# Row variance on one core: one row pitch for all loads, the first load at the head of SP's list

## The chip, the cores and the metric

The kernel runs on one core of a Trainium2 chip. The metric is the device time of one execution in microseconds; the median of several runs stands for a kernel. A profile is taken of one execution and shows its span, from the first to the last instruction that the profiler lists, with times from the span's start.

## The reference

For an input of 32 x 512 rows of 1024 float32 values (64 MiB) it computes one number per row, the variance as the mean of squares less the square of the mean.

```python
def reference(x: np.ndarray) -> np.ndarray:
    mean_sq = np.mean(x**2, axis=-1)
    sq_mean = np.mean(x, axis=-1)**2
    return (mean_sq - sq_mean).astype(np.float32)
```

## The kernel before

The 16384 rows are spread over 128 partitions. A "column" is one row on each of the 128 partitions, 512 KB in all. There are 128 columns, numbered 1 to 128. Columns 1 to 15 come from the first 128 x 15 rows of the input, so that neighbouring partitions read 15 rows (60 KB) apart; columns 16 to 128 come from the rest, with 113 rows (452 KB) between partitions. `src` (L83) forms these addresses.

Three SBUF slots of 16 columns each hold the input. Six main tiles (`MAIN`) go through them in turn, the first with 15 columns; then `TAPER` (L28) brings tile 6 and most of tile 7 in loads of 11, 7, 5, 4, 2, 1 and 1 columns, and `PIECES` (L38) the last two columns in halves and quarters of a row. All loads are issued by SP, in program order, through `load` (L126 to L132); a load into a slot that was used before waits until VectorE and ScalarE are done with it. Each load has a semaphore, or one shared by the tiles of a slot, and the engines wait for that.

Each column is done by one of two engines:

- VectorE runs `bn_stats` on the two half rows (L148, L151), or on the pieces (L316), which leaves counts, means and sums of squared deviations. They are brought together on GpSimd (POOL) for the main tiles and for the taper's loads marked "pool" (`aggregate`, `place`, L193 to L210), or on VectorE by `bn_aggr` (L143) for the last columns. A `bn_aggr` is held back in `held` and issued by `flush`, behind the next half row's `bn_stats`, so that its wait for the one before it costs less.
- ScalarE makes two passes (L160), one that accumulates the squares and one that accumulates the values; POOL's `combine` (L176, L177) then forms the variance.

`MAIN_BN` is the number of a main tile's 16 columns that VectorE takes, 11 of 16. One place in the main statistics is not used: column 0, which does not exist, and one column of tile 1 (`SPARE`), which ScalarE takes. A taper entry `(t, n, na, where)` is tile, columns, how many of them go to ScalarE, and where the rest is aggregated.

The results lie in `mv[:, 1, :]`. Two stores bring them out: `out_part` (L324), columns 1 to 15, 60 bytes per partition, as soon as the main aggregation is over; `out_rest` (L325), 452 bytes per partition, when POOL and VectorE are done. At the end SP waits for both.

Two instructions are moved by hand in the finished program (`move`): the first load, into the program's first block just ahead of SP's drain, so that it doesn't wait for the barrier that follows; and SP's last wait, into the last block.

Of the kernel before, what the change touches and what calls it, by code (L numbers as in the profile page):

```python
# [10 lines left out]
P = 128  # L11
D = 1024
HALF = 512
SLOT = 16
SLOTS = 3
MAIN = 6
MAIN_BN = 11


PART = SLOT - 1  # L20
REST = 8 * SLOT - PART
NCOLS = 1 + PART + REST

SPARE = (1, MAIN_BN - 1)

TAPER = [  # L28
    (6, 11, 5, "pool"),
    (7, 7, 2, "pool"),  # L30
    (6, 5, 2, "pool"),
    (7, 4, 1, "pool"),
    (7, 2, 1, "dve"),
    (7, 1, 0, "dve"),
    (7, 1, 1, "dve"),
]

PIECES = [  # L38
    (127, 0, 512),
    (127, 512, 512),  # L40
    (128, 0, 512),
    (128, 512, 256),
    (128, 768, 256),
]


# [27 lines left out]
def kernel(  # L74
# [3 lines left out]
):  # L78
    nc = tc.nc
    xf = x.flatten_outer_dims()  # L80
    assert tuple(xf.shape) == (P * (PART + REST), D)

    def src(c, n, e0=0, elems=D):  # L83
        row, pitch = (c - 1, PART) if c <= PART else (P * PART + c - 1 - PART, REST)
        return dataclasses.replace(
            xf, offset=row * D + e0, ap=[[pitch * D, P], [1, (n - 1) * D + elems]]
        )

    out_part = dataclasses.replace(out, offset=0, ap=[[PART, P], [1, PART]])
    out_rest = dataclasses.replace(out, offset=P * PART, ap=[[REST, P], [1, REST]])  # L90

    def sbuf(name, *shape):
        return nc.alloc_sbuf_tensor(name, [P, *shape], FP32).ap()

    slots = [sbuf(f"slot{i}", SLOT * D) for i in range(SLOTS)]
    last_column = sbuf("last_column", D)
    mv = sbuf("mv", 2, NCOLS)
    msq = sbuf("msq", NCOLS)
    n_late = sum(n - na for _, n, na, where in TAPER if where == "pool")
# [9 lines left out]
    dve = Stream(nc.vector, semaphore("dve"))  # L109
    act = Stream(nc.scalar, semaphore("act"))  # L110
    pool = Stream(nc.gpsimd, semaphore("pool"))
# [5 lines left out]
    def slot(t):  # L117
        return slots[t % SLOTS]

    def column(t, j, e0=0, n=D):  # L120
        return slot(t)[:, j * D + e0 : j * D + e0 + n]
# [4 lines left out]
    def load(dst, source, sem, *waits):  # L126
        for s, v in waits[:-1]:
            nc.sync.wait_ge(s, v)
        ins = nc.sync.dma_start(out=dst, in_=source)  # L129
        if waits:  # L130
            ins._wait_ge(*waits[-1])
        return ins.then_inc(sem, 16)  # L132
# [79 lines left out]
        )  # L212

    with tc.tile_critical(no_gpsimd_drain=True):  # L214
        for spare in (0, SPARE[0] * MAIN_BN + SPARE[1]):
            pool.step(lambda: nc.gpsimd.memset(stats_main[:, spare], 0.0))

        freed = []
        for t in range(MAIN):
            waits = freed[t - SLOTS] if t >= SLOTS else ()  # L220
            j0 = 1 if t == 0 else 0
            ins = load(
                slot(t)[:, j0 * D :],
                src(t * SLOT + j0, SLOT - j0),
                tile_sems[t % SLOTS],
                *waits,
            )
            if t == 0:
                early.append(ins.ins.name)
            landed = (tile_sems[t % SLOTS], 16 * (1 + t // SLOTS))  # L230
            first_d = first_a = (landed,)
            n_bn = MAIN_BN - (t == SPARE[0])
            for j in range(j0, SLOT):
                if j < n_bn:
                    last = bn_column(stats_main[:, t * MAIN_BN + j], column(t, j), *first_d)
                    first_d = ()
                    if j == n_bn - 1:
                        dve.step(last)
                    else:
                        last()  # L240
                else:
                    act_column(column(t, j), t * SLOT + j, *first_a)
                    first_a = ()
            freed.append((dve.done(), act.done()))

        main_dve, main_act = dve.done(), act.done()
        by_tile = "p (t k) -> p t k"
        cm = MAIN * SLOT
        mean_main = mv[:, 0, 0:cm].rearrange(by_tile, k=SLOT)
        var_main = mv[:, 1, 0:cm].rearrange(by_tile, k=SLOT)  # L250
        msq_main = msq[:, 0:cm].rearrange(by_tile, k=SLOT)
        combine(
            mean_main[:, :, MAIN_BN:],
            msq_main[:, :, MAIN_BN:],
            var_main[:, :, MAIN_BN:],
            (MAIN, SLOT - MAIN_BN),
            main_act,
        )
        qs, w = aggregate(stats_main, MAIN * MAIN_BN, "main", main_dve)
        place(var_main[:, :, :MAIN_BN], qs.rearrange(by_tile, k=MAIN_BN), w)  # L260
        c = SPARE[0] * SLOT + SPARE[1]
        combine(mv[:, 0, c : c + 1], msq[:, c : c + 1], mv[:, 1, c : c + 1], (1,))
        main_pool = pool.done()

        fill, late, end, placed = {}, 0, 0, []
        for i, (t, n, na, where) in enumerate(TAPER):
            k = fill.get(t, 0)
            fill[t] = k + n
            waits = freed[t - SLOTS] if k == 0 else ()
            c = t * SLOT + k  # L270
            load(
                slot(t)[:, k * D : (k + n) * D], src(c, n), taper_sems[i], *waits
            )
            landed = (taper_sems[i], 16)
            nb = n - na
            first = (landed,)
            for j in range(nb):
                if where == "pool":
                    last = bn_column(stats_late[:, late + j], column(t, k + j), *first)
                    if j == nb - 1:  # L280
                        dve.step(last)
                    else:
                        last()
                else:
                    stats = stats_end[:, end]
                    w = dve.step(bn_column(stats, column(t, k + j), *first))
                    hold_aggregate(c + j, stats[:, 0:2, :], w)
                    end += 1
                first = ()
            first = (landed,)  # L290
            for j in range(nb, n):
                act_column(column(t, k + j), c + j, *first)
                first = ()
            if na:
                a, b = c + nb, c + n
                combine(mv[:, 0, a:b], msq[:, a:b], mv[:, 1, a:b], (na,), act.done())
            if where == "pool":
                placed.append((c, late, nb))
                late += nb
                if late == n_late:  # L300
                    qs, w = aggregate(stats_late, n_late, "late", dve.done())
                    for c0, j0, m in placed:
                        place(mv[:, 1, c0 : c0 + m], qs[:, j0 : j0 + m], w)

        s = 0
        for i, (c, e0, n) in enumerate(PIECES):
            if e0 == 0:
                stats, s = stats_end[:, end], 0
                end += 1
            if c < 8 * SLOT:  # L310
                dst = column(7, c - 7 * SLOT, e0, n)
            else:
                dst = last_column[:, e0 : e0 + n]
            load(dst, src(c, 1, e0, n), piece_sems[i])
            w = dve.step(
                lambda: nc.vector.bn_stats(out=stats[:, s, :], in_=dst), (piece_sems[i], 16)  # L316
            )
            flush()
            s += 1
            if e0 + n == D:  # L320
                hold_aggregate(c, stats[:, 0:s, :], w)
        flush()

        load(out_part, mv[:, 1, 1 : 1 + PART], stored, main_pool)  # L324
        load(out_rest, mv[:, 1, 1 + PART :], stored, pool.done(), dve.done())  # L325
        end_wait = nc.sync.wait_ge(stored, 32).ins.name

    def move(program):


        blocks = program.main_func.blocks
        found = {}
        for b in blocks:
            for name in early + [end_wait]:
                for k, ins in enumerate(b.instructions):
                    if ins.name == name:
                        found[name] = ins
                        del b.instructions[k]
                        break
        sp = mybir.EngineType.SP  # L340

        def place_before_drain(block, names):
            at = next(
                k
                for k, ins in enumerate(block.instructions)
                if ins.engine == sp and isinstance(ins, mybir.InstDrain)
            )
            for name in reversed(names):
                block.instructions.insert(at, found[name])

        place_before_drain(blocks[0], early)
        place_before_drain(blocks[-1], [end_wait])

    nc.at_finalize(move)

# [29 lines left out]
```

## Time and profile before

| what | value |
|---|---|
| median of 9 runs | 165.34 us (165.13 to 165.83) |
| the profiled execution | 165.17 us |
| its span | 162.7 us |
| VectorE (DVE) busy | 102.3 us, 175 instructions |
| ScalarE (ACT) busy | 91.8 us, 173 instructions |
| GpSimd (POOL) busy | 12.2 us, 51 instructions |
| load of 15 columns, issue to landing | 21.0 us |
| last store, issue to landing | 1.6 us |
| read from HBM | 67.11 MB, mean 413 GB/s over the span |

The time of an execution is longer than its span by what lies around it, here 2.47 us. In the lists of the profile, DVE is VectorE, ACT ScalarE, POOL GpSimd, and SPq the queue of SP, which issues the DMAs. A row of the timeline gives start and duration in us, engine, line of the kernel, operation, the tiles that it writes and reads with their shapes, and in brackets how long the engine had been idle and what ended that. "L148" is line 148 of the kernel's file.

### The profile page before, as it was taken

How to read it: one execution, taken by the hardware profiler on the slowest of the kernel's cores; microseconds unless marked ns; L12 is line 12 of the kernel's file. 1: busy time of each engine (PE TensorE's matmuls, PEld its weight loads, DVE VectorE, ACT ScalarE, POOL GpSimd, SP SyncE). 2: the span in 40 equal slices, each digit the busy share in tenths (PEclk: the TensorE clock that was granted, in tenths of full speed). 3: DMA queues.
4: the chain of work that ended last, by engine and by line, in shares of the span. 5: the costliest groups of instructions: out<-in, count | busy, mean ns of one | idle time of the engine just before them, and what ended most of it. 6: DMA issues, size and time to landing. Idle time of an engine off the chain costs nothing.

```text
span 162.7 us, 477 instructions
## 1 busy us (share of the span) xinstructions
DVE 102.3 (63%) x175; ACT 91.8 (56%) x173; POOL 12.2 (8%) x51
## 2 busy tenths in 40 slices
DVE  0000089910998039990499706995099999698893
ACT  3000089700999039920499106980099669999780
POOL 0000000000000000000000000000000167000173
DMA  9999979979979989989998998998999999999970
GB/s 332 393 483 483 451 306 516 483 306 499 499 338 451 518 354 421 499 387 403 499 435 354 499 435 354 516 435 354 419 465 421 411 430 429 420 421 413 406 262 14
DMA packets 2882, 67.19 MB, mean 413 GB/s; under 512 B 576, under 2 KB 832, under 8 KB 1472
## 3 DMA queue, kind: packets, MB, share of 16 engines
q1 hardware_dynamic: 2880, 67.18, 96.5%
q14 instruction: 2, 0.02, 0.0%
HBM read 67.11 MB, written 0.07 MB: 413 GB/s over the span
## 4 chain that ended last, share of the span: by engine, by line
DMA 76%; DVE 10%; ACT 8%; POOL 3%; issue 1%; SPq 1%
DMA slot<-in_x_dram 76%; ACT scratch L160 8%; DVE stats_main L148 4%; DVE stats_main L151 4%; DVE stats_late L148 1%; DVE stats_late L151 1%; POOL mv L210 1%; SPq L129 0%; POOL mv L177 0%; POOL sqm L176 0%; POOL q_late L193 0%; POOL msb_late L199 0%; POOL qsb_late L203 0%; POOL msa_late L187 0%; POOL qsa_late L187 0%
## 5 line engine op out<-in xcount | busy, mean ns | idle before, releaser
L160 ACT ACTIVATE scratch<-slot 128x1024 f32<-128x1024 f32 x86 | 86.7, 1008 | 65.7 <-DMA slot<-in_x_dram 65.7
L148 DVE BATCH_NORM_STATS2 stats_main<-slot 128x6 f32<-128x512 f32 x64 | 43.4, 679 | 54.9 <-DMA slot<-in_x_dram 54.9
L151 DVE BATCH_NORM_STATS2 stats_main<-slot 128x6 f32<-128x512 f32 x64 | 43.3, 676 | 0.0
L160 ACT ACTIVATION_READ_ACCUMULATOR scratch<-slot 128x1 f32 x86 | 16.0, 186 | 0.0
L148 DVE BATCH_NORM_STATS2 stats_late<-slot 128x6 f32<-128x512 f32 x17 | 11.6, 681 | 2.8 <-DMA slot<-in_x_dram 2.7
L176 POOL TENSOR_TENSOR sqm<-mv 128x1 f32<-128x1 f32 (+3 forms) x8 | 1.6, 198 | 141.8 <-ACT scratch L160 141.8
L151 DVE BATCH_NORM_STATS2 stats_late<-slot 128x6 f32<-128x512 f32 x17 | 11.5, 676 | 0.0
L160 ACT ACT_TABLE_LOAD x1 | 1.3, 1283 | 0.9 <-SPq L214 0.9
L177 POOL TENSOR_TENSOR mv<-msq,sqm 128x1 f32<-128x1 f32 (+3 forms) x8 | 1.6, 198 | 0.6
L316 DVE BATCH_NORM_STATS2 stats_end<-last_column 128x6 f32<-128x256 f32 (+1 forms) x3 | 1.4, 486 | 0.0
L148 DVE BATCH_NORM_STATS2 stats_end<-slot 128x6 f32<-128x512 f32 x2 | 1.4, 676 | 0.0
L151 DVE BATCH_NORM_STATS2 stats_end<-slot 128x6 f32<-128x512 f32 x2 | 1.3, 658 | 0.0
L316 DVE BATCH_NORM_STATS2 stats_end<-slot 128x6 f32<-128x512 f32 x2 | 1.3, 658 | 0.0
L210 POOL TENSOR_SCALAR mv<-qsb_late 128x3 f32<-128x3 f32 (+2 forms) x4 | 0.8, 236 | 0.1
L143 DVE BATCH_NORM_AGGREGATE mv<-stats_end 128x2 f32<-128x12 f32 (+1 forms) x4 | 0.8, 204 | 0.0
L193 POOL TENSOR_TENSOR q_main<-stats_main 128x264 f32<-128x264 f32 x1 | 0.6, 645 | 2.1 <-DVE stats_main L151 2.1
L187 POOL TENSOR_TENSOR msa_main<-stats_main 128x132 f32<-128x132 f32 x1 | 0.6, 592 | 0.0
L187 POOL TENSOR_TENSOR vsa_main<-stats_main 128x132 f32<-128x132 f32 x1 | 0.6, 574 | 0.0
L187 POOL TENSOR_TENSOR qsa_main<-q_main 128x132 f32<-128x132 f32 x1 | 0.4, 404 | 0.1
L199 POOL TENSOR_SCALAR msb_main<-msb_main 128x66 f32<-128x66 f32 x1 | 0.4, 402 | 0.1
L203 POOL TENSOR_SCALAR qsb_main<-qsb_main 128x66 f32<-128x66 f32 x1 | 0.4, 392 | 0.1
L210 POOL TENSOR_SCALAR mv<-qsb_main 128x66 f32<-128x66 f32 x1 | 0.4, 386 | 0.1
(23 smaller groups left out, 5.3 us busy)
## 6 DMA issues: line engine op xcount, KB each, us to landing
slot<-in_x_dram SPq DMA_DIRECT2D x1, 7680.0 KB, 21.0
slot<-in_x_dram SPq DMA_DIRECT2D x1, 5632.0 KB, 38.8
slot<-in_x_dram SPq DMA_DIRECT2D x1, 3584.0 KB, 27.9
slot<-in_x_dram SPq DMA_DIRECT2D x1, 2560.0 KB, 33.7
slot<-in_x_dram SPq DMA_DIRECT2D x1, 2048.0 KB, 38.1
slot<-in_x_dram SPq DMA_DIRECT2D x1, 1024.0 KB, 40.1
slot<-in_x_dram SPq DMA_DIRECT2D x2, 512.0 KB, 41.3
slot<-in_x_dram SPq DMA_DIRECT2D x2, 256.0 KB, 41.9
```

Of the source, the lines that this page charges most:

```text
L143: lambda: dve.step(lambda: nc.vector.bn_aggr(out=mv[:, :, c], in_=stats), w)
L148: lambda: nc.vector.bn_stats(out=stats[:, 0, :], in_=xcol[:, 0:HALF]), *waits
L151: return lambda: nc.vector.bn_stats(out=stats[:, 1, :], in_=xcol[:, HALF:D])
L160: lambda: nc.scalar.activation(out=row, in_=xcol, func=func, scale=scale, accum_out=accum),
L176: w = pool.step(lambda: tt(out=sqm, in0=mean, in1=mean, op=ALU.mult), *waits)
L177: pool.step(lambda: tt(out=var, in0=meansq, in1=sqm, op=ALU.subtract), w)
L187: lambda: tt(out=a, in0=v[:, :, 0:2], in1=v[:, :, 2:4], op=ALU.add), *waits
L193: w = pool.step(lambda: tt(out=q, in0=mean, in1=mean, op=ALU.mult), *waits)
L199: lambda: ts(out=ms, in0=ms, scalar1=0.25, scalar2=None, op0=ALU.mult), w
L203: lambda: ts(out=qs, in0=qs, scalar1=256.0, scalar2=None, op0=ALU.mult), w
L210: lambda: ts(out=var, in0=qs, scalar1=1.0 / D, scalar2=None, op0=ALU.mult),
L316: lambda: nc.vector.bn_stats(out=stats[:, s, :], in_=dst), (piece_sems[i], 16)
```

## The change

- The rows are laid out as 128 per partition, with one pitch of 128 rows (512 KB) for all loads. `PART`, `REST`, the column 0 that does not exist and the buffer `last_column` go; the first load has 16 columns, and the last column lies in slot 1 with the rest of tile 7.
- In tiles 0 and 1, ScalarE takes 6 columns instead of 5 (`SPARE = 2`). In the taper, ScalarE takes 4 columns of the 11-column load instead of 5, and the fourth load has 3 columns instead of 4.
- One store of 512 bytes per partition replaces the two.
- The first load is inserted ahead of SP's first instruction in the first block, where before it stood ahead of SP's drain, behind SP's register moves.
- The aggregations on VectorE are held back by one step in both kernels.

```diff
+NCOLS = 8 * SLOT
...
-PART = SLOT - 1
-REST = 8 * SLOT - PART
-NCOLS = 1 + PART + REST
-
-SPARE = (1, MAIN_BN - 1)
+SPARE = 2
...
 TAPER = [
-    (6, 11, 5, "pool"),
+    (6, 11, 4, "pool"),
     (7, 7, 2, "pool"),
     (6, 5, 2, "pool"),
-    (7, 4, 1, "pool"),
+    (7, 3, 1, "pool"),
     (7, 2, 1, "dve"),
     (7, 1, 0, "dve"),
     (7, 1, 1, "dve"),
 ]
 
 PIECES = [
+    (126, 0, 512),
+    (126, 512, 512),
     (127, 0, 512),
-    (127, 512, 512),
-    (128, 0, 512),
-    (128, 512, 256),
-    (128, 768, 256),
+    (127, 512, 256),
+    (127, 768, 256),
 ]
...
     def src(c, n, e0=0, elems=D):
-        row, pitch = (c - 1, PART) if c <= PART else (P * PART + c - 1 - PART, REST)
         return dataclasses.replace(
-            xf, offset=row * D + e0, ap=[[pitch * D, P], [1, (n - 1) * D + elems]]
-        )
-
-    out_part = dataclasses.replace(out, offset=0, ap=[[PART, P], [1, PART]])
-    out_rest = dataclasses.replace(out, offset=P * PART, ap=[[REST, P], [1, REST]])
+            xf, offset=c * D + e0, ap=[[NCOLS * D, P], [1, (n - 1) * D + elems]]
+        )
+
+    out_pc = dataclasses.replace(out, offset=0, ap=[[NCOLS, P], [1, NCOLS]])
...
-        for spare in (0, SPARE[0] * MAIN_BN + SPARE[1]):
+        for t in range(SPARE):
+            spare = t * MAIN_BN + MAIN_BN - 1
             pool.step(lambda: nc.gpsimd.memset(stats_main[:, spare], 0.0))
...
-            j0 = 1 if t == 0 else 0
-            ins = load(
-                slot(t)[:, j0 * D :],
-                src(t * SLOT + j0, SLOT - j0),
-                tile_sems[t % SLOTS],
-                *waits,
-            )
+            ins = load(slot(t), src(t * SLOT, SLOT), tile_sems[t % SLOTS], *waits)
...
-            n_bn = MAIN_BN - (t == SPARE[0])
-            for j in range(j0, SLOT):
+            n_bn = MAIN_BN - (t < SPARE)
+            for j in range(SLOT):
...
-        load(out_part, mv[:, 1, 1 : 1 + PART], stored, main_pool)
-        load(out_rest, mv[:, 1, 1 + PART :], stored, pool.done(), dve.done())
-        end_wait = nc.sync.wait_ge(stored, 32).ins.name
+        load(out_pc, mv[:, 1, :], stored, pool.done(), dve.done())
+        end_wait = nc.sync.wait_ge(stored, 16).ins.name
...
-        place_before_drain(blocks[0], early)
-        place_before_drain(blocks[-1], [end_wait])
+        insert_before(blocks[0], mybir.Instruction, early)
+        insert_before(blocks[-1], mybir.InstDrain, [end_wait])
```

More of the change, by code (lines that the diff above doesn't have):

```diff
@@ L80 @@
     xf = x.flatten_outer_dims()
-    assert tuple(xf.shape) == (P * (PART + REST), D)
+    assert tuple(xf.shape) == (P * NCOLS, D)
     def src(c, n, e0=0, elems=D):
-        row, pitch = (c - 1, PART) if c <= PART else (P * PART + c - 1 - PART, REST)
         return dataclasses.replace(
-            xf, offset=row * D + e0, ap=[[pitch * D, P], [1, (n - 1) * D + elems]]
+            xf, offset=c * D + e0, ap=[[NCOLS * D, P], [1, (n - 1) * D + elems]]
         )
-    out_part = dataclasses.replace(out, offset=0, ap=[[PART, P], [1, PART]])
-    out_rest = dataclasses.replace(out, offset=P * PART, ap=[[REST, P], [1, REST]])
+    out_pc = dataclasses.replace(out, offset=0, ap=[[NCOLS, P], [1, NCOLS]])
     def sbuf(name, *shape):
@@ L95 @@
     slots = [sbuf(f"slot{i}", SLOT * D) for i in range(SLOTS)]
-    last_column = sbuf("last_column", D)
     mv = sbuf("mv", 2, NCOLS)
@@ L260 @@
         place(var_main[:, :, :MAIN_BN], qs.rearrange(by_tile, k=MAIN_BN), w)
-        c = SPARE[0] * SLOT + SPARE[1]
-        combine(mv[:, 0, c : c + 1], msq[:, c : c + 1], mv[:, 1, c : c + 1], (1,))
-        main_pool = pool.done()
+        j = MAIN_BN - 1
+        combine(
+            mean_main[:, :SPARE, j], msq_main[:, :SPARE, j], var_main[:, :SPARE, j], (SPARE,)
+        )
         fill, late, end, placed = {}, 0, 0, []
@@ L306 @@
         for i, (c, e0, n) in enumerate(PIECES):
+            j = c - 7 * SLOT
             if e0 == 0:
@@ L309 @@
                 end += 1
[L310 to L313, printed above, removed]
+            dst = column(7, j, e0, n)
             load(dst, src(c, 1, e0, n), piece_sems[i])
@@ L340, in move, with insert_before @@
         sp = mybir.EngineType.SP
-        def place_before_drain(block, names):
+        def insert_before(block, kind, names):
             at = next(
@@ L345, in place_before_drain @@
                 for k, ins in enumerate(block.instructions)
-                if ins.engine == sp and isinstance(ins, mybir.InstDrain)
+                if ins.engine == sp and isinstance(ins, kind)
             )
```

## The prediction

> **What bounds the kernel now.** I read the page's busy shares and its chain first, then the windows and the waits to see which stage is limited by what, then the timeline of the last 12 us, and at the last the packet records and semaphore landings that the trace keeps.
>
> ```profile
> span 162.7 us, 477 instructions
> ...
> DVE 102.3 (63%) x175; ACT 91.8 (56%) x173; POOL 12.2 (8%) x51
> ...
> q1 hardware_dynamic: 2880, 67.18, 96.5%
> ...
> DMA 76%; DVE 10%; ACT 8%; POOL 3%; issue 1%; SPq 1%
> ```
>
> No engine is near full, the load queue's packets fill 96.5% of sixteen DMA engines' span, and 76% of the chain that ended last is loads. The windows say how close that is to a ceiling (columns: window, its length, DVE, ACT and POOL busy with counts, clock, DMA share, GB/s):
>
> ```profile
> 20.00:60.00 40.00, 24.19 (x41) 23.33 (x45) 0.00 (x0) 1.00 1.00 434
> 60.00:100.00 40.00, 27.13 (x46) 21.82 (x43) 0.00 (x0) 1.00 1.01 436
> 156.00:158.50 2.50, 2.50 (x7) 2.19 (x4) 1.87 (x8) 1.00 0.61 204
> ```
>
> From 20 to 100 us the DMA engines have no gap (share 1.00) and move 434 to 436 GB/s. The packet records agree: 640 packets of 64 KB, mean 2.42 us, shortest 2.42, few above 2.45; one engine starts its next packet 2.414 us after the last. That is 1.207 us for a column of 128 rows. While VectorE needs 1.19 us for a column (two half rows each 0.59 apart) and ScalarE 2.08 us (two passes each 1.04 apart), both with fewer columns each than the loads bring, the loads set the pace. In the last window DVE is busy for 2.50 of 2.50 us: there the bound changes hands.
>
> ```profile
> 151.10 0.69 DVE L148 BATCH_NORM_STATS2 stats_late<-slot 128x6 f32<-128x512 f32 x1 [1.25 <-DMA slot<-in_x_dram]
> ...
> 158.38 0.68 DVE L316 BATCH_NORM_STATS2 stats_end<-last_column 128x6 f32<-128x512 f32 x1
> 158.97 0.19 DVE L143 BATCH_NORM_AGGREGATE mv<-stats_end 128x2 f32<-128x12 f32 x1
> 159.08 0.70 DVE L316 BATCH_NORM_STATS2 stats_end<-last_column 128x6 f32<-128x256 f32 x2
> ...
> 159.81 0.24 DVE L143 BATCH_NORM_AGGREGATE mv<-stats_end 128x2 f32<-128x18 f32 x1
> 160.02 0.19 POOL L177 TENSOR_TENSOR mv<-msq,sqm 128x1 f32<-128x1 f32 x1
> ```
>
> VectorE waits for a load at 151.10 for the last time and then runs without a gap to 160.05. The last five pieces land at 156.88, 157.53, 158.15, 158.45 and 158.76 (landings of their semaphores), but VectorE takes them up at 157.12, 157.82, 158.38, 159.08 and 159.37: it is behind by 0.24, 0.29, 0.23, 0.63 and 0.61 us. POOL ends later still, at 160.21, and SP's last store is issued at 160.28.
>
> **The change part by part.**
>
> *DMA as SP's very first instruction.* The span's first row is already this DMA at 0.00. The setup in the source is five register moves and one base load; in the instruction list that before compiles to they are gone, for nothing reads those registers, and the DMA heads SP's list. So the edit moves nothing: 0. Were the six there, SP's short instructions in the tail follow each other 0.06 to 0.07 us apart (160.87, 160.93, 161.00), so at most 0.4 us. I take 0. "Aggregations one step later" needs no price: `held` and `flush` stand in both kernels.
>
> *Columns per load.* The first load grows from 15 to 16 columns, the taper's fourth shrinks from 4 to 3; the total stays 128 columns, 154.5 us of the queue at 1.207. The ScalarE share goes from 5 to 4 in the 11-column load; tile 0 gets 6 columns on ScalarE (12.5 us) and 10 on VectorE (11.9), both far inside the 19.3 us of a tile. An extra POOL memset and a wider combine lie beside some 20 us of loads: 0.
>
> *The tail.* All loads from the 11-column one to the 5-column one land one column, 1.21 us, later against the stream's end; those after the fourth taper load stay where they are. VectorE: the 11-column load lands at 131.57 + 1.21 = 132.78, 7 columns of 1.19 end at 141.1; the next lands at 141.29, 5 columns end at 147.25; the next at 147.38, 3 columns end at 150.95; the fourth at 151.08 as before, now with 2 columns instead of 3: end 153.5, so the backlog of one column (1.19 us) is gone and each later load is met as it lands. The first half of the last column lands at 158.15, is taken up at 158.17 or 158.19 instead of 158.38, and from there the same rows follow: 1.67 us from 158.38 to 160.05. VectorE ends at 159.86. POOL: ScalarE finishes the fourth load at about 153.64 (its two columns of the 5-column load run from 147.38 to 151.55, then one column), the combine takes it to 154.2, the late aggregation takes 154.84 to 159.37 = 4.53 us now, so 158.75, then two combines of 0.46 and 0.41: 159.6. So VectorE becomes last, at 159.86 for 160.21: **-0.35 us**. Cover: VectorE has only 0.13 to 0.19 us of slack at each of these loads; if a load comes 0.2 us early, up to 0.2 of the gain goes.
>
> *The store.* Before, 128 runs of 60 bytes went out early; their packets lie at 156.83 to 158.37 behind the pieces in each ring, so dropping them moves no load (at most 8 x 0.011 = 0.09 us). The last store goes from 452 to 512 bytes per partition: 0.0266 us per packet by before's rows, 8 per engine, so +0.03 us at most, against -0.09. I take 0.
>
> *The row pitch.* All loads now step 512 KB from partition to partition, where before 15 columns stepped 60 KB and 113 stepped 452 KB. The trace has no 512 KB row. The two pitches it has read at one rate after the start: 2.267 us for 60 KB packets, 2.418 for 64 KB, both 27.1 GB/s per engine. Nearest is 452 KB, which costs nothing, and an engine already at the same ceiling under two pitches cannot gain: lower bound 0. The upper bound is the one slow place in the trace, the start, where all sixteen engines begin together: their first packets take 3.01 us on average for 2.267, an excess of 0.74. If a 512 KB pitch made the streams meet again once in each later 16 columns, that is 7 x 0.74 = 5.2 us. I take 0, by the 452 KB rows.
>
> The Trainium skill speaks against this change here: its page "DMA: Bandwidth & Descriptors", section "Latency and other measured facts", gives copies between HBM tensors at 512 KiB pitch 207 GB/s per direction where a padded pitch reached 214, and worse for larger powers of two; the aliasing that it names is an inference there. As an estimate from that page, 154.5 us would become 159.7, that is +5.2 us. No run here shows it: it is for copies, not for loads into SBUF, and before has no such pitch.
>
> *Sum.* The profiled execution took 165.17 us, 162.7 of span and 2.47 around it; -0.35 gives 164.82. It lies 0.17 below the median of 165.34, so on the median's scale: 165.0.
>
> **The rivals.**
>
> *The pitch slows the loads (slower).* Place: every load after the first. Price: 0.74 us for each 16 columns in which the engines collide once, so from 165.0 + 0.74 = 165.7 for one to 170.2 for seven, 167.6 for half. One suffices to outweigh the tail's 0.35. For it: with one common power of two step, sixteen engines that read in step have addresses that differ in high bits only, and the start shows that they can hamper each other. Against it: after their first packet the engines run staggered by some 1.1 us (their tile landings spread from 19.99 to 21.02) and keep the stagger to the end, and the trace shows almost no packet above its minimum, at 434 GB/s.
>
> *The tail gives nothing.* Which engine starts last at the start (1.00 to 1.75 us) and how long its first packet takes (2.65 to 3.40) sets the last landing; a different draw, or POOL staying last since ScalarE is later, gives 165.3, that is no change.
>
> *The first instruction does move.* 0.4 us more: 164.6.
>
> **How the numbers follow.** The forecast's case gets 0.45: the reads of two pitches at the ceiling and a tail that is worked out row by row. Its own range is 164.5 to 165.4. A measurement of this kernel can tell about 0.2% (0.33 us) from no change; the case's centre lies just on that bound, so 0.26 of it counts as faster, 0.19 as same. The pitch gets 0.43, because its bound is fifteen times the gain and nothing in before excludes it; all of it is slower. The tail that gives nothing gets 0.07 (0.04 same, 0.03 slower), the moved first instruction 0.05, faster. Together faster 0.31, same 0.23, slower 0.46. The range takes in the forecast's low end and the pitch's dearest sum: 164.5 to 170.2.
>
> **What would show it.** Right: 64 KB packets still at 2.42 us and 434 GB/s in the middle windows; VectorE waiting for a load at the last pieces (157.6, 158.2) rather than running through from 151; POOL ending before VectorE's last aggregate; SP's last store issued some 1.17 us after the last piece landed, where it was 1.52 (160.28 after 158.76). Wrong: middle windows below 430 GB/s or packets of 2.5 us and more, VectorE with longer waits for each tile, and a last piece that lands after 159.2. A span that grows at its start with SP's DMA further ahead of the other engines' first rows would show that the first edit is real.

## The result, and the profile after

The changed kernel takes 164.61 us (median of 9 runs, 164.50 to 165.09) for 165.39 us of the kernel before (29 runs): ratio 0.9957, interval 0.9947 to 0.9966. It is faster by 0.43%, or 0.78 us by the medians. The forecast was 165.0 us, a gain of 0.35. The two profiled executions differ by less than the medians: 164.61 against 165.17 us, spans 162.2 against 162.7. The profiled execution of before was one of its fastest.

First the page after: busy shares, the load queue, the chain.

```profile
span 162.2 us, 476 instructions
...
DVE 102.7 (63%) x175; ACT 91.7 (57%) x173; POOL 12.2 (8%) x51
...
q1 hardware_dynamic: 2736, 67.18, 96.8%
q14 instruction: 2, 0.02, 0.0%
...
DMA 78%; DVE 10%; ACT 8%; SPq 2%; issue 0%
```

The loads bound it as before. POOL, 3% of the chain before, is gone from it: it no longer ends last. The line for q14, two packets of instructions, was in before's page too; it is taken up again below. The same windows as for before:

```profile
20.00:60.00 40.00, 23.93 (x40) 25.16 (x48) 0.00 (x0) 1.00 1.00 431
60.00:100.00 40.00, 26.31 (x45) 21.00 (x41) 0.00 (x0) 1.00 1.00 434
...
156.00:158.50 2.50, 1.89 (x5) 2.19 (x4) 1.99 (x10) 1.00 0.66 233
```

The DMA share stays at 1.00 and the packets of 64 KB take 2.42 us at the new pitch as at the old ones: the streams are equally fast. (431 and 434 GB/s for 434 and 436 is no loss: the same windows of the kernels below lie between 428 and 441 at either pitch.) In the last window VectorE is busy for 1.89 us where it was for 2.50. The timeline of the tail shows why:

```profile
150.98 0.69 DVE L141 BATCH_NORM_STATS2 stats_late<-slot 128x6 f32<-128x512 f32 x1
...
156.72 0.69 DVE L303 BATCH_NORM_STATS2 stats_end<-slot 128x6 f32<-128x512 f32 x1 [0.61 <-DMA slot<-in_x_dram]
...
157.44 1.29 DVE L303 BATCH_NORM_STATS2 stats_end<-slot 128x6 f32<-128x512 f32 x2
...
158.65 0.19 DVE L136 BATCH_NORM_AGGREGATE mv<-stats_end 128x2 f32<-128x12 f32 x1
158.76 0.70 DVE L303 BATCH_NORM_STATS2 stats_end<-slot 128x6 f32<-128x256 f32 x2
...
159.30 0.19 POOL L170 TENSOR_TENSOR mv<-msq,sqm 128x1 f32<-128x1 f32 x1
159.50 0.24 DVE L136 BATCH_NORM_AGGREGATE mv<-stats_end 128x2 f32<-128x18 f32 x1
159.76 0.35 SPq L122 DMA_DIRECT2D out_dram<-mv  x1
```

VectorE waits 0.61 us for the first of the last pieces, so it has no backlog there. It ends at 159.73, POOL at 159.49, and SP issues the last store at 159.76 where it was 160.28: 0.52 us earlier. The store then takes 0.03 us less, which makes up the 0.55 us between the two spans. The time around the span is 2.45 us in both, and both spans begin with SP's first DMA.

### The profile page after: what moved, and what is told of

Same layout as the page of the kernel before. It is cut to its first block, busy times and chain, and to the rows that moved or that the text cites. A ratio compares the mean times of both kernels' runs of the same rounds, so it can differ in the third digit from the quotient of the medians.

```text
span 162.2 us, 476 instructions
## 1 busy us (share of the span) xinstructions
DVE 102.7 (63%) x175; ACT 91.7 (57%) x173; POOL 12.2 (8%) x51
## 4 chain that ended last, share of the span: by engine, by line
DMA 78%; DVE 10%; ACT 8%; SPq 2%; issue 0%
DMA slot<-in_x_dram 78%; ACT scratch L153 8%; DVE stats_main L141 4%; DVE stats_main L144 4%; SPq L122 2%; DVE stats_end L303 2%; DVE mv L136 0%; SPq L366 0%; SPq L121 0%; SPq L207 0%
## 5 line engine op out<-in xcount | busy, mean ns | idle before, releaser
L153 ACT ACTIVATE scratch<-slot 128x1024 f32<-128x1024 f32 x86 | 86.6, 1007 | 65.6 <-DMA slot<-in_x_dram 65.5
L169 POOL TENSOR_TENSOR sqm<-mv 128x2 f32<-128x2 f32 (+3 forms) x8 | 1.6, 199 | 142.1 <-ACT scratch L153 142.1
L303 DVE BATCH_NORM_STATS2 stats_end<-slot 128x6 f32<-128x512 f32 (+1 forms) x5 | 2.7, 566 | 0.6 <-DMA slot<-in_x_dram 0.6
L170 POOL TENSOR_TENSOR mv<-msq,sqm 128x2 f32<-128x2 f32 (+3 forms) x8 | 1.6, 200 | 0.6
L141 DVE BATCH_NORM_STATS2 stats_end<-slot 128x6 f32<-128x512 f32 x2 | 1.4, 694 | 0.0
L144 DVE BATCH_NORM_STATS2 stats_end<-slot 128x6 f32<-128x512 f32 x2 | 1.3, 658 | 0.0
L203 POOL TENSOR_SCALAR mv<-qsb_late 128x7 f32<-128x7 f32 (+3 forms) x4 | 0.8, 236 | 0.1
```

The costliest lines, as they stand in the source:

```text
L141: lambda: nc.vector.bn_stats(out=stats[:, 0, :], in_=xcol[:, 0:HALF]), *waits
L144: return lambda: nc.vector.bn_stats(out=stats[:, 1, :], in_=xcol[:, HALF:D])
L153: lambda: nc.scalar.activation(out=row, in_=xcol, func=func, scale=scale, accum_out=accum),
L169: w = pool.step(lambda: tt(out=sqm, in0=mean, in1=mean, op=ALU.mult), *waits)
L170: pool.step(lambda: tt(out=var, in0=meansq, in1=sqm, op=ALU.subtract), w)
L203: lambda: ts(out=var, in0=qs, scalar1=1.0 / D, scalar2=None, op0=ALU.mult),
```

## The experiments

All ratios are against the kernel before on the same chip, whose median was 165.69, 165.59 and 165.73 us in the three groups of runs. That varies by 0.08% between groups, so ratios are compared, not times. The diffs below show the main lines of each edit; entries of a list stand on one line, and `...` marks what is left out.

### The first load's place, and the stores

```diff
-        insert_before(blocks[0], mybir.Instruction, early)
+        insert_before(blocks[0], mybir.InstDrain, early)
```

> The changed kernel with its first load put back to where it stood before, ahead of SP's drain and behind SP's register moves. Theory (the edit is empty, since nothing reads those registers and the moves are dropped): 164.6 us as the changed kernel, ratio to before 0.9957, within 0.1 us; the span begins with SP's DMA at 0.00 and 2.45 us lie around it. Rival (the first load really came earlier, six short instructions of 0.06 to 0.07 us): 0.4 us slower than the changed kernel, 165.0 us, with the time around the span grown by as much.

Measured: ratio 0.9954 (0.9941 to 0.9968), the changed kernel's. The span begins with SP's DMA at 0.00, and 2.47 us lie around it. As far as the times can tell, the edit is empty.

```diff
-        load(out_pc, mv[:, 1, :], stored, pool.done(), dve.done())
+        load(out_part, mv[:, 1, :15], stored, main_pool)
+        load(out_rest, mv[:, 1, 15:], stored, pool.done(), dve.done())
```

> The changed kernel with its single store of 512 bytes per partition split as before into 60 bytes, issued early behind the main aggregation, and 452 bytes at the end. Tail theory: no effect on the loads, and 452 for 512 bytes at the end is worth under 0.05 us: 164.6 us (0.9955 to 0.996). Rival (the early store's 128 short packets disturb the last pieces, or stores under 512 bytes land later): 164.8 to 164.9 us, with the last piece landing 0.1 to 0.2 us later or the last store taking 1.6 us or more from issue to landing, for 1.56.

Measured: 0.9951 (0.9939 to 0.9964). One store or two makes no difference that can be told. The last piece lands 0.17 us later in its profile, at 158.85, which the rival had as a sign; but 0.16 us of that are there before any store goes out (21.43 for 21.27 in the table further down).

### The tail alone, put in and taken out

In before:

```diff
-    (6, 11, 5, "pool"), (7, 7, 2, "pool"), (6, 5, 2, "pool"), (7, 4, 1, "pool"),
+    (6, 11, 4, "pool"), (7, 8, 3, "pool"), (6, 5, 2, "pool"), (7, 3, 1, "pool"),
```

> The kernel before, two pitches and two stores kept, with VectorE's backlog taken out of the tail: the taper is (6,11,4), (7,8,3), (6,5,2), (7,3,1) in place of (6,11,5), (7,7,2), (6,5,2), (7,4,1), so that the last load for POOL's aggregation brings VectorE 2 columns instead of 3. Tail theory (the whole gain is there): VectorE waits again at the last pieces, ends at about 159.75, the last store is issued at about 159.8, and the time is 164.6 to 164.8 us (ratio 0.995 to 0.997). Layout theory (one pitch, the 16-column first load or the single store bring a part): the tail brings 0.35 as forecast, 165.0 us (0.998), and some 0.3 us stay missing against the changed kernel.

Measured: 0.9977 (0.9968 to 0.9985). That is the layout theory's 0.998: a part of the gain is missing. In its timeline VectorE waits again ahead of the last pieces:

```profile
157.47 0.69 DVE L316 BATCH_NORM_STATS2 stats_end<-slot 128x6 f32<-128x512 f32 x1 [0.60 <-DMA slot<-in_x_dram]
```

The last piece lands late in this profile, at 159.39 us for 158.76 in before's, so the store is issued at 160.47 in spite of the new tail. This profiled execution took 165.61 us, the longest of the kernel's eleven runs.

In the changed kernel:

```diff
-    (6, 11, 4, "pool"), (7, 7, 2, "pool"), (6, 5, 2, "pool"), (7, 3, 1, "pool"),
+    (6, 11, 5, "pool"), (7, 6, 1, "pool"), (6, 5, 2, "pool"), (7, 4, 1, "pool"),
```

> The changed kernel, one pitch and one store kept, with VectorE's backlog put back: the taper is (6,11,5), (7,6,1), (6,5,2), (7,4,1), 3 columns for VectorE in the fourth load as before. Tail theory: VectorE runs without a gap from 151 to 160.0, POOL ends at 160.1 to 160.2, and the time is 165.2 to 165.4 us (ratio 0.999 to 1.000). Layout theory: a part of the gain stays, 165.0 to 165.1 us (0.998).

Measured: 0.9977 (0.9968 to 0.9985) as well. VectorE has its backlog back, waits for a load for the last time at 151.51, and POOL ends last again:

```profile
151.51 0.69 DVE L141 BATCH_NORM_STATS2 stats_late<-slot 128x6 f32<-128x512 f32 x1 [1.23 <-DMA slot<-in_x_dram]
...
160.22 0.24 DVE L136 BATCH_NORM_AGGREGATE mv<-stats_end 128x2 f32<-128x18 f32 x1
160.44 0.19 POOL L170 TENSOR_TENSOR mv<-msq,sqm 128x1 f32<-128x1 f32 x1
160.70 0.35 SPq L122 DMA_DIRECT2D out_dram<-mv  x1
```

SP issues the store 0.94 us later than in the changed kernel's profile; 0.50 us of that are the last landing, at 159.18 for 158.68.

By the two ratios the tail theory, that all of the gain lies there, is wrong. The tail alone brings 0.23%, some 0.38 us, and the changed kernel without its tail keeps the other 0.23%. The two add up to 0.46%, for 0.43% and 0.46% measured on the whole change and on its first repetition.

### The layout: which pitch, and where

Before with one pitch, nothing else changed:

```diff
-        row, pitch = (c - 1, PART) if c <= PART else (P * PART + c - 1 - PART, REST)
+        row, pitch = c - 1, PART + REST
```

> The kernel before with nothing changed but the pitch: 128 rows (512 KB) for all its loads, the 15-column first load, the taper and the two stores kept. Half of the gain that the tail doesn't explain is to be placed. Pitch theory (60 KB or 452 KB between partitions costs time against 512 KB): ratio 0.9977, 0.4 us faster than before. Shape theory (the 15-column first load or the last column's own buffer costs it): 1.000.

Measured: 0.9975 (0.9965 to 0.9984). The rows' layout alone brings what the tail leaves open; the 15-column first load and the last column's own buffer do not cost it.

The changed kernel with two pitches again, 16 and 112 rows:

```diff
+        row, pitch = (c, 16) if c < 16 else (P * 16 + c - 16, NCOLS - 16)
         return dataclasses.replace(
-            xf, offset=c * D + e0, ap=[[NCOLS * D, P], [1, (n - 1) * D + elems]]
+            xf, offset=row * D + e0, ap=[[pitch * D, P], [1, (n - 1) * D + elems]]
```

> The changed kernel with its 16 columns in the first load and its taper kept, but the rows in two parts again, 16 and 112 per partition (64 KB between partitions in the first load, 448 KB in the others), and so two stores. Pitch theory: the 0.4 us come back, ratio 0.998 to 0.9985. Shape theory: 0.9955 as the changed kernel with two stores.

Measured: 0.9942 (0.9930 to 0.9954), no loss at all. Two pitches as such cost nothing, and neither theory covers both results. What is left is the split in 15 and 113: 60 KB between partitions in the first load, or 452 KB in the others.

The two trade places: still 15 and 113, but the 15-row part becomes the sixth tile, and the first load is 16 columns at 452 KB:

```diff
-        row, pitch = (c - 1, PART) if c <= PART else (P * PART + c - 1 - PART, REST)
+        if C0 < c < C0 + SLOT:          # C0 = 80, the sixth tile's column that does not exist
+            row, pitch = c - C0 - 1, PART
+        else:
+            row, pitch = P * PART + (c if c < C0 else c - SLOT), REST
```

> The kernel before, still in parts of 15 and 113 rows, but with the 15-row part (60 KB between partitions) loaded as the sixth tile and the first load made of 16 columns of the 113-row part (452 KB). Taper, backlog of VectorE and early store of the 15-row part kept. Start theory (it is the first load at 60 KB between partitions: the DMA engine that later takes VectorE's instruction fetch begins with a packet that is 0.2 to 0.9 us longer, and it lands last): ratio 0.9975 as with one pitch, and that engine's first packet is within 0.7 to 0.9 us of its later ones. Pitch theory (452 KB or 60 KB between partitions slows loads wherever they stand): 1.000.

Measured: 0.9954 (0.9942 to 0.9967). The gain is there, with the pitches of before and VectorE's backlog of before; it is larger than the 0.9975 expected. So what costs is the first load at 60 KB between partitions, and not a pitch in the stream. How much it costs isn't settled: 0.25% by the one kernel, 0.46% by the other, on two chips. The second sign of the start theory was just missed: the first packet of the engine in question took 0.93 us more than its later ones, for 0.7 to 0.9 expected.

### Which engine ends last: the instruction fetches

The page of before has a second queue:

```profile
q14 instruction: 2, 0.02, 0.0%
```

These are two packets of 8 KB, at 53.84 and 63.68 us. They bring instructions, share the sixteen DMA engines with the loads, and each holds one engine up: its own 0.31 us, and 0.29 and 0.58 us more on the load packet that follows it. The traces also suggest whose they are. In all thirteen kernels without added ScalarE work one fetch comes when ScalarE has begun 48 to 56 of its recorded instructions, and in all thirteen without added VectorE work one comes when VectorE has begun 50 to 56. In before the earlier is ScalarE's and the later VectorE's. An engine can be followed through the packet records, since each 64 KB packet begins where that engine's last one ended. For the engine that takes the second fetch, the table gives when it finished the first load (15 columns counted as 16, that is 8 x 0.151 us later) and when the kernel's last piece landed.

| kernel | first load, step between partitions | that engine's end of the first load | last landing | difference |
|---|---|---|---|---|
| before | 60 KB | 21.39 | 158.76 | 137.37 |
| before, new tail | 60 KB | 22.02 | 159.39 | 137.37 |
| before, half of the main work | 60 KB | 21.92 | 159.31 | 137.39 |
| changed | 512 KB | 21.27 | 158.68 | 137.41 |
| changed, two stores | 512 KB | 21.43 | 158.85 | 137.42 |
| changed, half of the main work | 512 KB | 21.32 | 158.75 | 137.42 |
| before, one pitch | 512 KB | 21.33 | 158.76 | 137.43 |
| changed, 16 and 112 rows | 64 KB | 21.18 | 158.62 | 137.44 |
| before, first load at 452 KB | 452 KB | 21.36 | 158.80 | 137.44 |

Nine profiles, and the last landing follows this one engine to 0.07 us. In three others, whose load packets were slower here and there in the stream, the difference is 137.53 to 137.88; the last two, below, have a third fetch. The engine is followed by times alone, and where engines end their packets within a few thousandths of a microsecond of each other it can be taken for a neighbour: in the row "before, one pitch" the possible ends of the first load run from about 21.0 to 21.4, so that row is weak. In the two rows with a late engine only one reading fits.

With 60 KB the engine is late in two of three profiles, by 0.5 to 0.8 us; its first packet took 1.61 and 1.51 us above 2.27, in before's own profile 0.99 or 1.07 (two engines end it within 0.002 us of each other). That profile looks like a lucky draw, and its time was the second lowest of 29. How often the engine is late can't be told from three profiles, of which one is its kernel's longest run.

Two kernels were to take the fetches away, by leaving out half of the main tiles' work, so that their output is no longer the variance:

```diff
-                    act_column(column(t, j), t * SLOT + j, *first_a)
+                    act_pass(column(t, j), ACTF.Square, 1.0 / 32.0, ...)
...
+                if j < n_bn - 1 and t in (1, 2):
+                    continue
```

> The changed kernel with work left out in the main tiles, so that VectorE and ScalarE have under 128 instructions each: VectorE does one half of each row and of tiles 1 and 2 one column alone, ScalarE only the pass of squares. Loads, taper and stores are as they were. Fetch theory: the two 8 KB instruction fetches that the trace shows at 53 and 64 to 67 us on the DMA engines, each of which holds one engine up by 0.6 to 0.9 us, are gone; in the changed kernel that engine ended only 0.05 us behind the next, so 164.4 to 164.7 us (ratio 0.994 to 0.9955). Without such a role of the fetches: 0.9955.

> The kernel before with the same work left out (one half of each row on VectorE in the main tiles, of tiles 1 and 2 one column alone; only the pass of squares on ScalarE). Fetch theory: in before the engine that took the second fetch landed last, 0.44 us behind the next one, and so set the end; without fetches 0.3 to 0.5 us faster, ratio 0.997 to 0.998, and what is left between this and the changed kernel with the same work left out is the tail's 0.35. If the pitch itself costs 0.4 us: no change, 1.000, or as much less as the changed kernel gains.

Measured: 0.9943 (0.9927 to 0.9959), within the expected range, and 0.9985 (0.9975 to 0.9995), outside it. The fetches did not go, so the first is no proof; with fewer instructions per tile they came later, at 86.6 and 124.7 us and at 104.7 and 122.3 us. By the counts above the earlier is ScalarE's and the later VectorE's. Both kernels also lost 0.34 us around the span (2.11 for 2.45 us), which is more than their gain over the kernels that they were made from. So they don't test what they were made for, and give two rows of the table.

The opposite, one more fetch for VectorE:

```diff
+        for i in range(60):
+            nc.vector.memset(junk[:, i : i + 1], 0.0)
```

> The changed kernel with 60 more VectorE instructions (memsets of one element per partition into a buffer that nothing reads) before its first data has landed, so that VectorE's instruction list is fetched once more within the span. Fetch theory (VectorE's fetches go through one DMA engine, and that engine's lateness is the end of the loads): the second fetch holds the same engine up once more by 0.6 to 0.9 us, the last piece lands at 159.2 to 159.5 and the time is 165.2 to 165.5 us (ratio 0.999 to 1.001). Rival (a fetch is spread or hidden, and the last landing has another cause): 164.6 us, 0.9955.

Measured: 0.9969 (0.9958 to 0.9980), 165.22 us. Its DMA part has the third fetch:

```profile
q14 instruction: 3, 0.02, 0.0%
```

The fetches at 9.2 and 123.9 us fall on the same engine, that at 55.3 on another. The last piece lands at 159.62, a little beyond the 159.2 to 159.5 expected and 0.94 us later than in the changed kernel, and the span is 163.1 for 162.2. Again the time around the span is shorter, 2.13 us, so that the time grew by 0.61 (165.22 for 164.61 in the two profiled runs). The rival's 0.9955 lies just outside the interval, and the later landing says more: a further fetch of VectorE delays the end of the loads, as the fetch theory has it. The 165.22 us lie at the low end of the expected 165.2 to 165.5, but the ratio missed its 0.999 to 1.001, by what changed outside the span.

And one more for ScalarE:

```diff
+                    make = lambda: nc.scalar.activation(out=junk[:, i : i + 1], ...)   # 30 times, behind tile 0
```

> The changed kernel with 60 more ScalarE instructions (30 passes over one element per partition, each with its read of the accumulator, into buffers that nothing reads) behind its first tile, so that ScalarE's instruction list is fetched once more within the span. Fetch theory: ScalarE's fetches go through another DMA engine than VectorE's, one that ended earlier, so two of them cost less than two of VectorE's: 164.7 to 165.2 us, ratio 0.996 to 0.999. Rival (any further fetch costs the same, or none does): as the kernel with 60 more VectorE instructions, or 0.9955.

Measured: 0.9961 (0.9949 to 0.9974), in the expected range but not to be told from the changed kernel. Its two ScalarE fetches, at 40.7 and 123.7 us, may fall on one engine (the packet records allow another reading too), and the last landing is at 159.16. In this profile load packets were slow at several places, so the share of the fetches in that is open.

### A faster tail

```diff
-    (126, 0, 512), (126, 512, 512),
-    (127, 0, 512), (127, 512, 256), (127, 768, 256),
+    (126, 0, 256), (126, 256, 384), (126, 640, 384),
+    (127, 0, 384), (127, 384, 384), (127, 768, 256),
```

> The changed kernel with the last two columns in six pieces of 256, 384, 384 and 384, 384, 256 elements for five of 512, 512 and 512, 256, 256. Tail theory: VectorE idles 0.61 us before the first piece, so a smaller first piece starts its last chain earlier and it ends 0.1 to 0.2 us sooner: 164.45 us, ratio 0.994 to 0.995. Rival (one more bn_stats of 0.06 us fixed cost and smaller packets eat it): 0.9955 as the changed kernel.

Measured: 0.9939 (0.9927 to 0.9952), the lowest ratio of all, though its interval overlaps the changed kernel's. VectorE's wait ahead of the pieces is halved:

```profile
156.67 0.43 DVE L304 BATCH_NORM_STATS2 stats_end<-slot 128x6 f32<-128x256 f32 x1 [0.31 <-DMA slot<-in_x_dram]
...
159.69 0.24 DVE L137 BATCH_NORM_AGGREGATE mv<-stats_end 128x2 f32<-128x18 f32 x1
```

It ends 0.91 us after the last landing (159.01) where the changed kernel needs 1.05 (159.73 after 158.68). That 0.14 us lies within the 0.1 to 0.2 expected. It beats the kernel before clearly; that it beats the changed one is likely by the profile and not shown by the times.

## Why the prediction was right, and where it was not

**The forecast and its chances.** The forecast, 0.35 us faster, had the direction right and less than half of the size, and the chances did not favour it: slower had 0.46, faster 0.31. The range of 164.5 to 170.2 was wide because it took in the rival of the slow pitch, so that the time lies in it says little. The range of the forecast's own case, 164.5 to 165.4, says more; the time lies 0.11 us above its low end, and that it came so low is due to a term that the forecast did not have.

**The tail: right.** The chain was worked out row by row: POOL no longer last, VectorE meeting the last pieces as they land, VectorE's end at 159.86. It came at 159.73, 0.13 us earlier, as the last column's first half landed 0.13 us earlier (158.02 for 158.15). The store was issued 1.08 us after the last landing, for 1.17 forecast. The tail's -0.35 us is borne out by the runs that isolate it: 0.23% or 0.38 us, put in or taken out. A term was missed in SP's hand-over: with POOL last, SP waited for POOL ahead of the store and issued it 0.07 us after POOL's end; with VectorE last it is 0.03 us. These parts and the 0.03 us of the store, 0.35 + 0.13 + 0.04 + 0.03, make up the 0.55 us between the two profiled spans.

**The first instruction: right at 0.** Undone, it changed nothing.

**The stores: right at 0.**

**The row pitch: the step that failed.** The sum put 0 for it, with 0 as its lower bound: engines at one ceiling under two pitches cannot gain. That holds for the stream, where packets take 2.42 us at 448, 452 and 512 KB. It does not hold for the start, and the start was in the trace: the first packets' excess of 0.74 us served as the price of collisions at the new pitch, and the sum did not ask whether it depends on the old one. The runs without a first load at 60 KB between partitions show that the term should have been -0.25% or more, some 0.4 us or more; it is the half of the gain that the forecast lacks. How the step acts is shown in part: in two of the three profiles at 60 KB the engine that later takes VectorE's instruction fetch begins late, and it lands last. That this lateness is the whole of what the medians lose is argued from these few profiles and not shown.

**The rival that the pitch slows the loads: wrong.** 431 and 434 GB/s in the middle windows, no repeated collision. The Trainium skill's row on HBM row pitch at large powers of two ("DMA: Bandwidth & Descriptors", section "Latency and other measured facts") did not apply: its copies between HBM tensors ran at 207 GB/s per direction at 512 KiB where a padded pitch gave 214. The loads of 64 KB runs into SBUF lost nothing here, with 2.42 us per packet at 452 and at 512 KB. The chance of 0.43 rested on a bound alone, with nothing in before's stream that pointed to it.

**The rival that the tail gives nothing** named the right quantity, which engine starts late and how long its first packet takes, but as a draw of equal engines. One of them counts more: in before it pays 0.89 us (0.31 and 0.58) for a fetch later on.

**The base: a draw of its own.** The sum started from an execution of 165.17 us and added 0.17 to come to the median's scale. By the account above, that difference was itself an effect of the start, which the change removes, so that it should not have been added; no run shows this alone.

What stays open: why the first packet of that engine is longer at 60 KB than at 64, 452 or 512 KB. Three profiles at 60 KB and one engine are all there is; other steps were not tried. Open, too, is why the two kernels that keep before's tail and take the first load off 60 KB differ, with 0.25% and 0.46%. Also open is why VectorE work at the very start shortens the time around the span by 0.33 us.

## What to carry to other kernels

When loads run at the engines' ceiling, look at the engine that lands last and at what it did besides: here its start and one 8 KB instruction fetch set the end, while the averages of the stream were equal. A tail is worth working out row by row, engine by engine, from landings: the forecast of VectorE's end was off by 0.13 us, as much as the last column's first half landed earlier. One profiled execution is one draw; compare its time with the median before taking its smallest terms for the kernel's.

## What the runs showed of the hardware that was not expected

- Instruction fetches of 8 KB go through the same DMA engines as the loads. One holds its engine up by its own 0.31 us and by 0.24 to 0.66 us on the load packet that follows it. In the kernel with two fetches of VectorE both fell on one engine.
- The first load's step between partitions decided 0.25 to 0.46% of the time while the later packets took 2.42 us in all kernels: 60 KB was the slow one, and no loss was seen at 64, 452 and 512 KB.
- The time around the span was 2.45 to 2.48 us in eleven kernels and 2.11 to 2.13 us in the three where VectorE had work ahead of the first load's landing.
